# A gated MLP's up-projection as seven half-size products instead of eight

## The chip, the cores and the metric

The kernel runs on one core of one Trainium2 chip. The metric is the device time of one execution in microseconds (us); the number for a kernel is the median of its runs. One execution was also taken with the hardware profiler, and every row below is from that one.

## What is computed

Two trunk layers act on 640 tokens (128 context tokens and 512 latent tokens) of width 1024. Each layer is a mixer followed by a gated MLP with a depthwise convolution of width 3 over the tokens between its up-projection and its activation. The part that matters here:

```python
D_FF = ((8 * D_MODEL // 3 + 127) // 128) * 128      # 2816 = 22 chunks of 128
FFN_CONV = 3
...
def conv_ffn(h, p):
    u = dwconv(h @ p['ffn_w_up'], p['ffn_conv_w'], p['ffn_conv_b'])
    val, gate = jnp.split(u, 2, axis=-1)
    return (jax.nn.silu(gate) * val) @ p['ffn_w_down']
```

All data is fp32. The kernel multiplies with a split: each operand is the sum of a high part in the fp32r format and a low part, and a product is three matmuls (weight high times input high, weight high times input low, weight low times input high) that are accumulated in PSUM.

## The kernel before, in words

The program is written by a planner. Python generators emit the instructions; a class `Clock` keeps an estimated time for each engine, and `pick` gives an elementwise step to whichever of two engines would be through first by those estimates. The estimates hold a cost for each instruction alone. `Engine` records every operation, so that all instructions carry the line of its call (L175) in the profile, and the groups go by tile names.

The main stream is a list of jobs in order. Beside it run threads (`spawn`) that consume the results. `Stream` (`ws`) loads the weights: a unit is 128 x 1024 values; `raw` is its landing place (two buffers, `NRAW`), ScalarE (ACT) makes the high part `wh`, and VectorE (DVE) or GpSimd (POOL) subtracts to make the low part `wl`. There are three buffers of each (`NSPLIT`), loads run up to two units ahead of the splits, and a raw buffer is free again as soon as its one split is done.

In the MLP the normalised input lies feature-major in `h_hi` and `h_lo`: 8 blocks of 128 features by 642 columns (128 context tokens, two zero columns, 512 latent tokens). `up` makes the 44 chunks of 128 output features, a value chunk `j` and then its gate chunk `22 + j`. A chunk is one `fm_job`: 8 blocks times 3 matmuls on two pieces of columns, 258 and 384 wide (`PIECES`), into two PSUM banks, 48 matmuls in all. `up_then` consumes them: `conv` reads the PSUM banks (first tap on ACT or DVE, the two other taps as DVE scalar_tensor_tensor), then Silu on the gate, the product of value and gate, and a split into `act_hi` and `act_lo`. The chunks are made in `GROUPS` of 8, 8 and 6 pairs; after each group `down` (and `down_last`) multiplies its part of the activations with the down weights, in two halves of 512 output columns, and `add_gated` adds the result to the residual. `fm_primed` runs the first chunks of a layer in column stages, as the normalised tiles come.

PSUM has 8 banks, of which up to 6 (`MCAP`) serve products of the main stream.

Of the kernel before, what the change touches and what calls it, by code (L numbers as in the profile page):

```python
# [9 lines left out]
F32 = mybir.dt.float32  # L10
# [5 lines left out]
NT = 642  # L16
EPS = 1e-6
GROUPS = ((0, 8), (8, 16), (16, 22))
# [41 lines left out]
class Clock:  # L60
    """estimated times of the engines, for the order in which instructions are emitted"""
# [49 lines left out]
    def free(self, n):  # L111
        """when the last user of a tile is done"""
# [18 lines left out]
ROWS = {"xT": NT, "s0": 2, "sh0": 2, "h_hi": NT, "h_lo": NT, "C456": 384}  # L131


def tnames(xs):
    """what the waits go by: tiles, or the rows of the tiles that are worked on in parts"""
# [13 lines left out]
class Slots:  # L149
    """a pool whose tiles take over the waits of the tiles that had their place"""  # L150
# [92 lines left out]
def kernel(ctx: ExitStack, tc: tile.TileContext, a: dict, o: dict):  # L243
# [27 lines left out]
    # PSUM tiles and token-major tiles are taken and given back in emission order, so that no engine waits for a later one  # L271
# [4 lines left out]
    def get(kind, n=1, keep=0):  # L276
# [13 lines left out]
        pool = pl["tok" if kind == "tok" else "gn"].real  # L290
# [77 lines left out]
    def slot_free(tag, bufs):  # L368
        """when the next tile of the tag is free"""
        L = strm.names.get(tag, [])  # L370
        return clk.free(L[-bufs]) if len(L) >= bufs else 0.0

    class Stream:
        """units of the products' weights: loads run NRAW ahead of the splits, splits tn.look ahead of the products"""

        def __init__(self):
            self.desc, self.got, self.on = [], {}, False
            self.n_dma = self.n_split = self.n_take = self.n_done = 0

        def pump(self, force=False):  # L380
            while self.on:
                now, i = clk.now(), self.n_split
                if i < min(self.n_dma, self.n_take + tn.look, self.n_done + NSPLIT) and (
                        force or slot_free("wh", NSPLIT) <= now and clk.free(tname(self.got[i])) <= now + 0.5):
                    raw, n = self.got[i], self.desc[i][1]
                    hi = strm.tile([128, 1024], F32R, tag="wh", name="wh", bufs=NSPLIT)
                    lo = strm.tile([128, 1024], F32R, tag="wl", name="wl", bufs=NSPLIT)
                    ACT.activation(hi[:, :n], raw[:, :n], AF.Copy)
                    eng = DVE if pick(clk.last, DVE=n / 960 + tn.lobias, POOL=n / 460) == "DVE" else POOL
                    eng.tensor_tensor(lo[:, :n], raw[:, :n], f(hi[:, :n]), ALU.subtract)  # L390
                    self.got[i] = (hi, lo)
                    self.n_split += 1
                    continue
                i = self.n_dma
                if i < min(len(self.desc), self.n_split + NRAW) and (force or slot_free("raw", NRAW) <= now + 0.5):
                    src, n = self.desc[i]
                    t = strm.tile([128, 1024], F32, tag="raw", name="raw", bufs=NRAW)
                    SP.dma_start(t[:, :n], src)
                    self.got[i] = t
# [11 lines left out]
        def done(self, n=1):  # L411
            self.n_done += n
# [18 lines left out]
    def load_x(key, src):  # L431
        """the residual stream stays out of SBUF while the mixer needs the room"""
# [1476 lines left out]
```

## Time and profile before

| | us |
|---|---|
| median of 3 runs | 1764.34 |
| lowest and highest run | 1763.33, 1765.52 |
| span of the profiled execution, first to last instruction | 1752.2 |
| PE busy in it | 1661.6 |
| DVE, ACT, POOL busy in it | 1009.3, 718.5, 537.4 |

The profiled execution's own time is not given apart from its span; the median lies 12.1 us above the span. PE is TensorE's matmul stream, PEld its weight loads, which overlap it. Matmul records overlap one another, since matmuls are pipelined: the pace of a stretch is read from start to start, not from the length of a record. The MLP of the first layer runs from about 412 to 890 us, that of the second from about 1275 us to the end.

### The profile page before, as it was taken

The numbers are of one execution on the slowest core, as the hardware profiler recorded it, in microseconds if no ns is written. First come the engines' busy times: TensorE is split into PE (matmuls) and PEld (weight loads), VectorE is DVE, ScalarE is ACT, GpSimd is POOL, SyncE is SP. The second block draws the span as 40 slices with busy tenths as digits, with TensorE's granted clock in tenths as the row PEclk, the third lists the DMA queues.
The fourth block names the chain that finished last, engine by engine and source line by source line (L and its number), as shares of the span: only waits on it lengthen the run. The fifth ranks groups of instructions, "written<-read, shape, count | busy, mean of one in ns | idle before, by whom it ended". The sixth has DMA issues, their size and how long they took to land.

```text
span 1752.2 us, 25505 instructions
## 1 busy us (share of the span) xinstructions
PE 1661.6 (95%) x10192; PEld 1485.5 (85%) x10192; DVE 1009.3 (58%) x1866; ACT 718.5 (41%) x1136; POOL 537.4 (31%) x344
## 2 busy tenths in 40 slices
PE   6897999999999999999999899999899999999997
PEld 5787878768997999799789876887799989998996
DVE  5467987677443344344464779877854434443445
ACT  6466435426332233223274765443453313331333
POOL 1334653322331233123123355442213212321331
PEclk9998999999999999999999999999999999999999
DMA  8424555533223222322533355643122321222222
GB/s 326 121 49 81 128 179 174 187 109 103 73 73 108 64 82 73 96 73 73 180 121 107 75 135 158 181 166 105 60 73 73 87 81 61 73 85 72 73 85 84
DMA packets 62668, 188.63 MB, mean 108 GB/s; under 512 B 9550, under 2 KB 17734, under 8 KB 62550
## 3 DMA queue, kind: packets, MB, share of 16 engines
q1 hardware_dynamic: 62550, 187.01, 34.7%
q8 instruction: 80, 1.31, 0.3%
q14 instruction: 38, 0.31, 0.1%
HBM read 180.46 MB, written 6.52 MB: 107 GB/s over the span
## 4 chain that ended last, share of the span: by engine, by line
PE 72%; DVE 14%; ACT 4%; DMA 4%; issue 3%; POOL 1%; SPq 0%; POOLq 0%; DVEq 0%; ACTq 0%
PE at L175 72%; DVE tok L175 5%; DVE x L175 2%; DMA wg<-in_wlru 2%; DVE gt L175 1%; DVE sp L175 1%; DVE C L175 1%; DMA tok<-cTd 1%; ACT L175 1%; DVE lb L175 1%; ACT xn L175 1%; ACT hf L175 1%; POOL wl L175 1%; DMA araw<-in_w_ada 1%; ACT lb L175 1%
## 5 line engine op out<-in xcount | busy, mean ns | idle before, releaser
L175 POOL TENSOR_TENSOR wl<-raw,wh 128x1024 fp32r<-128x1024 f32 (+3 forms) x167 | 388.3, 2326 | 946.7 <-ACT wh L175 883.2
L175 PE MATMUL at<-h_hi,wh 128*128 128x258 f32 (+2 forms) x1912 | 599.9, 314 | 5.0 <-ACT wh L175 3.9
L175 PE MATMUL at<-h_hi,wl 128*128 128x258 f32 (+2 forms) x1912 | 590.4, 309 | 5.6 <-POOL wl L175 4.8
L175 PE MATMUL at<-h_lo,wh 128*128 128x258 f32 (+2 forms) x1912 | 590.0, 309 | 0.5 <-DVE h_lo L175 0.5
L175 PEld LDWEIGHTS at<-h_hi,wh 128*128 128x128 f32 x1912 | 363.7, 190 | 20.1 <-issue 5.2
L175 PEld LDWEIGHTS at<-h_hi,wl 128*128 128x128 f32 x1912 | 362.8, 190 | 6.9 <-POOL wl L175 5.9
L175 PEld LDWEIGHTS at<-h_lo,wh 128*128 128x128 f32 x1912 | 364.1, 190 | 2.6 <-DVE h_lo L175 0.7
L175 ACT ACTIVATE wh<-raw 128x1024 fp32r<-128x1024 f32 (+3 forms) x210 | 212.7, 1013 | 223.1 <-PE at L175 168.1
L175 DVE SCALAR_TENSOR_TENSOR cv<-at,par,cv 128x258 f32<-128x258 f32 (+1 forms) x352 | 185.9, 550 | 71.4 <-ACT cv L175 59.6
L175 ACT ACTIVATE cv<-at,par 128x258 f32<-128x258 f32 (+1 forms) x130 | 76.5, 601 | 317.4 <-PE at L175 317.4
L175 PE MATMUL at<-wh,h_hi 128*128 128x384 f32 (+2 forms) x480 | 184.9, 385 | 2.3 <-DVE tok L175 1.4
L175 PE MATMUL at<-wl,h_hi 128*128 128x384 f32 (+2 forms) x480 | 172.6, 359 | 2.7 <-POOL wl L175 2.7
L175 PE MATMUL at<-wh,act_hi 128*128 128x512 f32 x440 | 174.3, 396 | 0.0
L175 PE MATMUL at<-wl,act_hi 128*128 128x512 f32 x440 | 173.6, 395 | 0.6 <-POOL wl L175 0.6
L175 PE MATMUL at<-wh,act_lo 128*128 128x512 f32 x440 | 173.4, 394 | 0.0
L175 PE MATMUL at<-wh,h_lo 128*128 128x384 f32 (+2 forms) x480 | 172.5, 359 | 0.0
L175 DVE TENSOR_SCALAR cv<-at,par 128x384 f32<-128x384 f32 x46 | 31.2, 677 | 188.3 <-PE at L175 188.3
L175 DVE TENSOR_TENSOR gt<-at,gate 128x512 f32<-128x512 f32 x100 | 68.4, 684 | 104.2 <-PE at L175 104.2
L175 ACT ACT_TABLE_LOAD x87 | 111.6, 1283 | 21.9 <-PE at L175 13.6
L175 PEld LDWEIGHTS at<-wh,h_hi 128*128 128x128 f32 x480 | 91.3, 190 | 28.4 <-issue 12.6
L175 PEld LDWEIGHTS at<-wh,act_hi 128*128 128x128 f32 x440 | 82.7, 188 | 24.0 <-issue 3.4
L175 PEld LDWEIGHTS at<-wl,h_hi 128*128 128x128 f32 x480 | 91.2, 190 | 12.2 <-POOL wl L175 3.5
(169 smaller groups left out, 1903.1 us busy)
## 6 DMA issues: line engine op xcount, KB each, us to landing
raw<-in_wup SPq DMA_DIRECT2D x88, 512.0 KB, 3.5
araw<-in_w_ada SPq DMA_DIRECT2D x80, 512.0 KB, 4.5
raw<-in_wdn SPq DMA_DIRECT2D x44, 512.0 KB, 3.5
raw<-in_wfm SPq DMA_DIRECT2D x28, 512.0 KB, 3.6
ar<-in_wada SPq DMA_DIRECT2D x16, 512.0 KB, 10.2
tok<-cTd SPq DMA_DIRECT2D x40, 192.0 KB, 4.6
raw<-in_wout SPq DMA_DIRECT2D x14, 512.0 KB, 3.5
x<-in_xin SPq DMA_DIRECT2D x10, 512.0 KB
```

Source lines behind the costliest of these rows:

```text
L175: res = real(*args, **kw)
```

## The change

The up-projection of a pair of chunks (value chunk `j` and gate chunk `22 + j`) is done as one 2 x 2 block product. The blocks of the input are two halves of the columns (`NH` = 322; the tiles are widened to 644 columns) by two halves of the features (four blocks of 128 each); the blocks of the weights are the two feature halves by value and gate. The direct way is 8 block products. The new way is the Winograd form of Strassen's product: 7 block products, each of 4 blocks times 3 matmuls on 322 columns.

- `sums` makes the sums of input blocks once per layer, and their splits `s1`, `s2`, `s4` in a new pool `S`; `s3` takes the place of a block of `h_hi` and `h_lo`.
- `Stream.prep` makes the weights of the seven products from the two raw tiles of a pair, half a unit (512 columns) each: four more sums (`T1`, `T2` in two steps, `T4`), and seven splits. The sums are made in place, so both raw tiles stay taken until the last of the seven (`T4`) is prepared; `n_rel` then rises by two and the next two loads may go. Six buffers `w` hold high and low part of one product each.
- `pair_job` runs the seven products in three PSUM banks. Partial results are copied out by ACT (`snap`), added on DVE (`out`) into an SBUF tile `C`, and the accumulation goes on in the same bank.
- The convolution (`conv_sb`) now reads SBUF, with 642 columns at once. `product` is the old product of value and gate.
- The first two pairs of each layer stay as chunks: three in `fm_primed` in both layers (before: two in the first layer, three in the second), and one `fm_job`. 20 pairs per layer go the new way.
- `GROUPS` are now 6, 6, 4 and 6 pairs.

```diff
-GROUPS = ((0, 8), (8, 16), (16, 22))
+GROUPS = ((0, 6), (6, 12), (12, 16), (16, 22))
+NH = 322
...
     class Stream:
+        OPS = ("11", "T1", "T2", "22", "T3", "21", "T4")
...
+        def slot(self, name):
+            self.slots += 1
+            return strm.tile([128, 1024], F32R, tag="w", name=name, bufs=2 * NSPLIT)
+
+        def prep(self, op, i):
...
+            v, g = self.raws[i], self.raws.get(i + 1)
+            t = self.slot("wp")
+            hi, lo = t[:, 0:512], t[:, 512:1024]
+            a, c, b, d = (x_ and x_[:, s_] for x_ in (v, g) for s_ in (slice(0, 512), slice(512, 1024)))
+
+            def tt(*args):
+                (DVE if pick(clk.last, DVE=0.9, POOL=1.25) == "DVE" else POOL).tensor_tensor(*args)
+
+            if op == "T1":
+                src = pl["ffn"].tile([128, 512], F32, tag="t1", name="t1")
+                tt(src, b, a, ALU.subtract)
+            elif op == "T2":
+                tt(b, d, b, ALU.subtract)
+                tt(a, b, a, ALU.add)
+                src = a
+            elif op == "T4":
+                tt(c, c, a, ALU.subtract)
+                src = c
+            else:
+                src = {"11": a, "22": d, "T3": b, "21": c}[op]
+            ACT.activation(hi, src, AF.Copy)
+            eng = DVE if pick(clk.last, DVE=0.6 + tn.lobias / 2, POOL=1.25) == "DVE" else POOL
+            eng.tensor_tensor(lo, src, f(hi), ALU.subtract)
+            if op == "T4":
+                self.n_rel += 2
+                del self.raws[i], self.raws[i + 1]
+            return hi, lo
...
+                    if (last < self.n_dma and self.slots + ns <= self.freed + 2 * NSPLIT
+                            and (self.n_split < self.n_take + (tn.look if op == "w" else 5)) and (
+                            force or slot_free("w", 2 * NSPLIT, ns) <= now
+                            and clk.free(tname(self.raws[last])) <= now + 0.5)):
...
-                if i < min(len(self.desc), self.n_split + NRAW) and (force or slot_free("raw", NRAW) <= now + 0.5):
+                if i < min(len(self.loads), self.n_rel + NRAW) and (force or slot_free("raw", NRAW) <= now + 0.5):
...
+        def sums():
...
+            for t_, k0, c in ((t11, 0, c0), (t12, 4, c0)):
+                tt(t_, f(h_hi[:, k0:k0 + 4, c]), f(h_lo[:, k0:k0 + 4, c]), ALU.add)
...
+            for t_, k0 in ((t22, 4), (t21, 0)):
+                tt(t_, f(h_hi[:, k0:k0 + 4, c1]), f(h_lo[:, k0:k0 + 4, c1]), ALU.add)
...
+            def put(n, src):
+                s_hi, s_lo = S[n]
+                ACT.activation(s_hi, src, AF.Copy)
+                clk.dep = clk.last
+                tt(s_lo, src, f(s_hi), ALU.subtract)
+
+            tt(t22, t22, t21, ALU.add)
+            put("s1", t22)
...
+            tt(cc, t11, t21, ALU.subtract)
+            tt(t11, t22, t11, ALU.subtract)
+            put("s2", t11)
...
+            tt(t12, t12, t11, ALU.subtract)
+            put("s4", t12)
...
+        def conv_sb(dst, src, w):
+            if pick(ACT=0.8, DVE=0.55) == "ACT":
+                ACT.activation(dst, src, AF.Identity, scale=w[:, 1:2], bias=w[:, 3:4])
+            else:
+                DVE.tensor_scalar(dst, src, w[:, 1:2], w[:, 3:4], ALU.mult, ALU.add)
+            yield
+            DVE.scalar_tensor_tensor(dst[:, 1:NT], src[:, 0:NT - 1], w[:, 0:1], dst[:, 1:NT], ALU.mult, ALU.add)
+            DVE.scalar_tensor_tensor(dst[:, 0:NT - 1], src[:, 1:NT], w[:, 2:3], dst[:, 0:NT - 1], ALU.mult, ALU.add)
+
+        def pair_job(j, g0):
...
+            def mul(b, a, start):
+                a_hi, a_lo = S[a]
+                hi, lo = ws.take()
+                ps = bank[b][:, 0:NH]
+                for k in range(4):
+                    for w_, h_, first, last in ((hi, a_hi, k == 0 and start, False), (hi, a_lo, False, False), (lo, a_hi, False, k == 3)):
+                        PE.matmul(ps, w_[:, 128 * k:128 * k + 128], h_[:, k, :], start=first, stop=last, skip_group_check=True)
...
+            def snap(n, b):
+                e = ev[n] = ffn.tile([128, NH], F32, tag=n, name="e")
+                ACT.activation(e, bank[b][:, 0:NH], AF.Copy)
...
+            def out(half, part, b, n, free):
...
+                if n is not None:
+                    DVE.tensor_tensor(dst, src, ev[n][:, 0:w], ALU.add)
...
+                if (half, 1 - part) in ev:
+                    spawn(tail(half))
+
+            def tail(half):
...
+                yield from conv_sb(cc, c, P("cf", l, 22 * half + j))
...
+            bank["P"], = yield from get("mm")
+            yield from mul("P", "a11", True)
+            run_(snap("e1", "P"))
+            bank["V"], = yield from get("mm")
+            yield from mul("V", "s1", True)
+            run_(snap("e5", "V"))
+            yield from after("e1")
+            yield from mul("P", "s2", False)
+            run_(snap("e2", "P"))
+            yield from after("e5")
+            yield from mul("V", "s4", False)
+            run_(out(1, 0, "V", "e2", True))
+            yield from after("e2")
+            yield from mul("P", "s3", False)
+            run_(out(1, 1, "P", "e5", False))
+            bank["Q"], = yield from get("mm")
+            yield from mul("Q", "a12", True)
+            run_(out(0, 0, "Q", "e1", True))
+            yield from after((1, 1))
+            yield from mul("P", "a22", False)
+            run_(out(0, 1, "P", None, True))
```

## Rows read from the trace of the kernel before

**Rows 1.** The page, its first part: busy us, share of the span, instructions.

```profile
PE 1661.6 (95%) x10192; PEld 1485.5 (85%) x10192; DVE 1009.3 (58%) x1866; ACT 718.5 (41%) x1136; POOL 537.4 (31%) x344
```

**Rows 2.** The chain that ended last: start, us, what; its two longest pieces.

```profile
411.99 454.02 PE at L175 x2760
...
1274.83 425.70 PE at L175 x2630
```

**Rows 3.** Busy us by stretch: length, PE, PEld, DVE, ACT, POOL, PEclk, DMA share, GB/s.

```profile
405.00:412.00 7.00, 4.96 (x36) 4.19 (x34) 6.93 (x7) 6.29 (x14) 4.07 (x3) 1.00 0.29 80
...
586.00:643.00 57.00, 57.00 (x387) 57.00 (x386) 25.28 (x44) 17.62 (x25) 16.79 (x7) 1.00 0.27 84
```

**Rows 4.** Timeline of PE, one block of a chunk: start, us, instruction.

```profile
460.13 0.28 PE L175 MATMUL at<-h_hi,wh 128*128 128x258 f32 x1
...
460.48 0.34 PE L175 MATMUL at<-h_hi,wh 128*128 128x384 f32 x1
...
461.01 0.29 PE L175 MATMUL at<-h_hi,wh 128*128 128x258 f32 x1
```

**Rows 5.** Timeline of ACT over one pair of chunks.

```profile
484.70 0.57 ACT L175 ACTIVATE cv<-at,par 128x258 f32<-128x258 f32 x1 [4.96 <-PE at L175]
...
489.92 0.74 ACT L175 ACTIVATE act_hi<-cv 128x642 fp32r<-128x642 f32 x1 [0.89 <-DVE cv L175]
...
498.92 0.57 ACT L175 ACTIVATE cv<-at,par 128x258 f32<-128x258 f32 x1 [4.96 <-PE at L175]
```

**Rows 6.** Timeline of DVE over the same pair.

```profile
486.01 2.18 DVE L175 SCALAR_TENSOR_TENSOR cv<-at,par,cv 128x258 f32<-128x258 f32 x4
...
490.69 0.83 DVE L175 TENSOR_TENSOR act_lo<-cv,act_hi 128x642 fp32r<-128x642 f32 x1 [0.81 <-ACT act_hi L175]
```

**Rows 7.** Timelines of POOL and DVE in two stretches where both work.

```profile
1306.36 2.41 POOL L175 TENSOR_TENSOR wl<-raw,wh 128x1024 fp32r<-128x1024 f32 x1 [4.76 <-ACT wh L175]
...
1305.37 2.19 DVE L175 SCALAR_TENSOR_TENSOR cv<-at,par,cv 128x258 f32<-128x258 f32 x4 [3.08 <-ACT cv L175]
1307.47 1.98 DVE L175 TENSOR_TENSOR act_lo<-cv,act_hi 128x642 fp32r<-128x642 f32 x1
...
399.75 1.19 POOL L175 TENSOR_TENSOR h_lo<-hf,h_hi 128x512 fp32r<-128x512 f32 x1 [21.48 <-ACT h_hi L175]
...
399.84 1.66 DVE L175 TENSOR_TENSOR x<-x,gt 128x512 f32<-128x512 f32 x1
...
401.86 0.69 DVE L175 TENSOR_TENSOR h_lo<-hf,h_hi 128x512 fp32r<-128x512 f32 x1
```

**Rows 8.** By tile and by shape: count, duration ns (min/median/max, or busy and mean).

```profile
L175 DVE SCALAR_TENSOR_TENSOR lb<-lb x16: 818/828/2284, 70.6 to 1076.1; 128x642 f32<-128x642 f32 x16
...
L175 DVE SCALAR_TENSOR_TENSOR cv<-at,par,cv x352: 475/548/622, 426.2 to 1702.9; 128x258 f32<-128x258 f32 x88, 128x383 f32<-128x383 f32 x88
...
L175 DVE TENSOR_TENSOR tok<-tok,at 128x384 f32<-128x384 f32 x28 | 14.2, 547 | 4.6 <-PE at L175 3.9 <-POOL tok L175 0.7
```

**Rows 9.** Timelines of ACT and DVE: a half unit's and a whole unit's split steps.

```profile
411.22 0.63 ACT L175 ACTIVATE h_hi<-hf 128x512 fp32r<-128x512 f32 x1
...
485.16 1.05 ACT L175 ACTIVATE wh<-raw 128x1024 fp32r<-128x1024 f32 x1
...
417.54 1.23 DVE L175 TENSOR_TENSOR wl<-raw,wh 128x1024 fp32r<-128x1024 f32 x1
```

**Rows 10.** DMA issues, KB, us to landing: the page, then 861.9 to 863 us.

```profile
raw<-in_wup SPq DMA_DIRECT2D x88, 512.0 KB, 3.5
...
araw<-in_w_ada SPq DMA_DIRECT2D x2, 512.0 KB, 4.4
raw<-in_wdn SPq DMA_DIRECT2D x1, 512.0 KB, 5.2
```

**Rows 11.** Timeline of PE where an up group ends and down begins.

```profile
699.39 0.34 PE L175 MATMUL at<-h_hi,wl 128*128 128x384 f32 x1
699.57 0.40 PE L175 MATMUL at<-wh,act_hi 128*128 128x512 f32 x1
```

More of the change, by code (lines that the diff above doesn't have):

```diff
@@ L380, in pump @@
         def pump(self, force=False):
             while self.on:
[L382 to L393, printed above, removed]
+                now = clk.now()
@@ L1558, in ffn_jobs, with cv_tile @@
         cur = {}
+        def cv_tile(j, half):
+            while cur.get("mult", -1) < j - 1 if half else cur.get("split", -1) < j - 2:
+                yield
+            return pl["ffn"].tile([128, NT], F32, tag=f"cv{half}", name="cv", bufs=2 - half)
         def up_then(j, g0, half):
             def then(ps, rel_):
-                cc = pl["ffn"].tile([128, NT], F32, tag=f"cv{half}", name="cv", bufs=2)
+                cc = yield from cv_tile(j, half)
                 yield from conv(cc, ps, P("cf", l, 22 * half + j), 1, rel_)
@@ L1569, in then, with product @@
                 yield
-                val = cur["cv", j, 0]
-                DVE.tensor_tensor(val, val, cc, ALU.mult)
-                yield
-                a_hi, a_lo = cur["act", g0]
-                split(a_hi[:, j - g0, :], a_lo[:, j - g0, :], val)
-                yield
-                cur["done", j] = True
-            return then
+                yield from product(j, g0, cur["cv", j, 0], cc)
+            return then
+        def product(j, g0, val, gate):
+            DVE.tensor_tensor(val, val, gate, ALU.mult)
+            cur["mult"] = j
+            yield
+            while ("act", g0) not in cur:
+                yield
+            a_hi, a_lo = cur["act", g0]
+            split(a_hi[:, j - g0, 0:NT], a_lo[:, j - g0, 0:NT], val)
+            cur["split"] = j
+            yield
+            cur["done", j] = True
@@ L1579, in begin_group, with act_tiles @@
+        def act_tiles():
+            return [pl["ffn"].tile([128, 6, 2 * NH], F32R, tag=f"a_{nm}", name=nm) for nm in ("act_hi", "act_lo")]
         def begin_group(g0, g1):
             def fn():
-                cur["act", g0] = [pl["ffn"].tile([128, g1 - g0, NT], F32R, tag=f"a_{nm}", name=nm, padded_shape=[128, 8, NT])
-                                  for nm in ("act_hi", "act_lo")]
-            return fn
+                while g0 == 0 and "sums" not in cur:
+                    yield
+                cur["act", g0] = act_tiles()
+            return fn
@@ L1593, in up @@
-            for j in range(j0, g1):
-                for half in range(1 if g0 == 0 and j == 1 and TUNE[2 * l + 1]["npr"] > 2 else 0, 2):
-                    add_fm(a["wup"][l, 22 * half + j], up_then(j, g0, half))
+                add_fm(a["wup"][l, 23], up_then(1, g0, 1))
+                hook(lambda: cur.update(plain=True))
+            else:
+                hook(lambda: run_now(begin_group(g0, g1)()))
+            for j in range(max(g0, 2), g1):
+                job([("pair", a["wup"][l, j], a["wup"][l, 22 + j])], lambda j=j: pair_job(j, g0))
@@ L1597, in down, with run_now @@
+            if g1 == 22:
+                hook(lambda: pl.exit("S"))
+                hook(lambda: pl.enter("nb", f"nc{l}", side="right"))
+        def run_now(gen):
+            for _ in gen:
+                raise AssertionError
         def down(g0, g1, hf):
```

142 lines of the change are left out of this document (122 added, 20 removed).

## The prediction, made before the changed kernel had been run

> **What bounds the kernel now.** I read the busy shares first, then the chain of waits, then the busy times by stretch, then the timelines of one pair of chunks. PE is busy 1661.6 of 1752.2 us [rows 1], and the two longest pieces of the chain that ended last are PE alone, 454 and 426 us, which are the two MLPs [rows 2]. Inside an up group PE is busy 57.00 of 57.00 us, with DVE at 25.3, ACT at 17.6 and POOL at 16.8 [rows 3]. So in the MLP a shorter matmul stream is worth its full length, as long as the other three engines keep up; they look less than half loaded. A share of 57 us hides which of their steps can run at the same time, and that is where I think this change is decided.
>
> The pace: one block of a chunk, six matmuls, takes 460.13 to 461.01 = 0.88 us, three of 258 columns in 0.35 and three of 384 in 0.53 [rows 4]. That is 0.117 and 0.177 us each, 0.45 and 0.46 ns a column, so time goes with columns. A pair of chunks takes 498.92 - 484.70 = 14.22 us [rows 5].
>
> **PE's part of the change.** A pair had 96 matmuls with 2 x 24 x 642 = 30816 columns; it gets 7 x 12 = 84 with 84 x 322 = 27048. At 14.22 us for 30816 columns that is 12.5 us, or 1.79 for each of the seven products. A width of 322 lies between the two that I can see. 40 pairs would save 40 x 1.74 = 70 us if PE never waited. The Trainium skill (TensorE: Matmul & The Clock Gate, section Back-to-back issue gap) gives an isolated warm gap of N/2.4 + 2.5 ns; by it the saving would be 64 us. The rows are slower than that rule (117 against 110 ns for 258 columns), and I go by the rows.
>
> **The port that DVE and POOL share.** POOL ran a subtraction from 1306.36 for 2.41 us. A DVE subtraction with both inputs in SBUF was issued at 1307.47 and took 1.98 us instead of 0.83: it ended 0.68 us behind POOL's end. The conv steps just before, which have one input in PSUM, ran beside POOL at their usual 2.19 for four. Again at 399.75: POOL 1.19, DVE 1.66 instead of 0.69, ending 0.56 behind [rows 6, 7]. The grouped rows say the same: the conv's step on PSUM never took over 622 ns in 352 cases, the step with two SBUF inputs took 818 to 2284 [rows 8]. So here a POOL subtraction and a DVE step on two SBUF tensors exclude each other for their whole length. The Trainium skill (SBUF — State Buffer, section Who interferes with whom) states this rule, an exclusive lock on a shared port, and it speaks against this change. Without it DVE and POOL would work side by side and the pair would be bound by PE at 12.5; with it the sums below hold. The trace agrees.
>
> Now the pair's steps that need that port. The conv moves from PSUM to SBUF: four 642-wide steps with two SBUF inputs, plus product and activation split as before, six in all, each 0.68 us of port (0.83 as a DVE step) [rows 6 to 8]. Weights: seven low-part subtractions and four sums, eleven half-width steps, 0.56 us of port on DVE (0.69 as a step) or 1.19 on POOL [rows 7]. First taps, if DVE takes them, I count at 0.35. With x of the eleven on DVE the port needs 4.4 + 0.56x + 1.19(11 - x). Before, the same sum was 2 x 0.68 + 2 x 2.41 = 6.2 of 14.2. DVE itself has six steps at 0.83, three adds from PSUM at about 0.5 (547 ns for 384 columns [rows 8]), about 1 of copies and first taps, and 0.69x. x = 11 gives 10.6 of port but 15.1 of DVE; x = 0 gives 17.5 of port. The planner's estimates do not know the port; they favour DVE by 0.15 to 0.35 us when both engines are free, so I take x = 7: 13.1 of port, 12.3 of DVE. No split of the steps lets the pair go at 12.5, and none is far below 13. ACT has seven half-width copies at 0.63, three snaps near 0.6, Silu, split and up to two first taps at 0.74 [rows 5, 9]: at most 9.2, no bound.
>
> **The loop through the raw buffers.** Before, a raw tile came free after one split, and loads ran ahead. Now both tiles of a pair stay taken until T4 is split, and only then go the next two loads. One load lands in 3.5 us, the last of three that were issued together in 5.2 [rows 10]. Then the weight steps follow one another: T1 = 0.69 + 0.63 + 0.69 = 2.0, T2 with two sums 2.7, the splits of 22, T3 and 21 one behind another 1.9, T4 2.0 [rows 7, 9]; with handing over 8.8. The loop is 5.2 + 8.8 = 14.0 us if nothing else is on the port. Six 0.83 steps of the pair that is being multiplied (5.0 us) and POOL's longer steps compete in it; some fall into the load's gap and into T1's, T2's and T4's waits on ACT. Ends: 12.3 (a load of 3.5, nothing else in the way) and 19.0 (all six in the way). I take 16.5, half of the 5.0 in the way, because the DVE queue is in order and the planner, which believes in a shorter loop, puts these steps between each other.
>
> A group's first pair is prepared during the down stage. T4 of its first pair is done at about 4 us (its first product, then 2.0), of the second at 4 + P, and the third pair can run its third product 5.2 + 4.7 behind that, with five products of 1.79 to go: it ends at P + 22.9. A group of six takes 4P + 22.9, one of four 2P + 22.9. Four pairs, six, four and six in each layer: 12P + 91.4. P = 16.5 gives 289 against 20 x 14.25 = 285 before: +9 us for both layers. Ends: P = 14 gives -51, P = 19 gives +69. It breaks even at 16.1.
>
> **From up to down.** Before, PE goes from the last up matmul to the first down matmul without a gap, 699.39 to 699.57 [rows 11]. Now the first down unit is loaded only after the last T4: 3.5 + 1.05 + 2.41 (1.23 on DVE) = 5.8 to 7.0 us [rows 7, 9, 10], while PE has about 4.5 us of products left. Stall 1.3 to 2.5, at eight places, and more if these steps queue: I take 20, ends 0 and 24.
>
> **Head of each MLP.** Twelve sums and subtractions of 1288 columns, by the rows' slope (0.83 at 642, 1.23 at 1024) 1.5 us each on DVE, 3 on POOL; nine of them come after the last norm, 13.6 us, with 9 of conv steps and some 4 of weight steps on the same queue: 26 us. PE covers 72 matmuls of 256 columns (8.5), one chunk (7.1) and three products (5.4): 21. I take 6 a layer, 12 us; ends 0 and 26. The norms there already keep DVE at 6.93 of 7 us [rows 3], so the two early sums do not come free either.
>
> **Other parts, at nothing.** Ten more gate additions a layer (a fourth group) lie beside down matmuls, where PE alone is late; twenty times two steps of 0.69 = 28 us if that cover were gone. Loads are the same bytes. PE's clock: the granted level stayed at 1.00 with PE busy 4.96 of 7 us [rows 3], so PE waits of this size should not lower it.
>
> **Sum.** +9 + 20 + 12 = +41 us. The profiled span is 1752.2; the median lies 12.1 above it and I keep that: 1764.3 + 41 = 1805.
>
> **Rivals.**
> - *The port packs tightly (faster).* T4's steps get through early and the tails fall into the load's gap: P near the port's 13.1, 20 x 13.1 = 261 a layer, -48; half the stalls at the transitions and heads, +16: 1732. Past P = 16.1 it turns. For it: PE's saving is certain, and ACT and the load gap leave room. Against: the measured exclusion.
> - *The queue couples loop and products (slower still).* The last product of a pair accumulates in a bank that `out(1, 1)` must have read on DVE; if that step is queued behind the next pair's first subtraction, which waits for its load, PE waits for a DMA in every pair. P goes to 19: +69 and both upper ends, +119: 1883.
> - *The two sides cancel.* P near 14.5 to 15 (-39 to -27) with the 32 us of stalls: 1757 to 1769, about the old time.
> - *The new width does not pay.* If 322-column matmuls ran at the pace of 384 (0.177 us), PE would need 14.9 a pair; the two widths seen scale, so I give this no chance of its own.
>
> **How the numbers follow.** Forecast case 0.52 (1805; own range 1772 to 1850), slower still 0.12, cancel 0.07, tight 0.29. Within 0.2%, about what a measurement of this kernel can tell from no change, falls nearly all of the cancelling case. So faster 0.30, same 0.07, slower 0.63. The cases have both signs, so the range spans from the tight case's middle to the far end of the slow one: 1728 to 1880.
>
> **What the profile after would show.** Right: in the up groups PE is busy about 75 to 85% and waits for the weight tiles (`wp`, `w`), whose releasers are DVE or POOL subtractions; pairs come every 16 to 17 us; loads of `in_wup` come in twos, each pair of issues just behind a T4 split; DVE steps on `cv` with two SBUF inputs show maxima near 2 us; a gap of 1 to 3 us at each start of down. Wrong: PE busy over 95% there and pairs every 13 us (the tight case), or PE's waits ending at `snap` or `out` rather than at weights, or a gap at the heads of over 15 us.

## The result, and the profile after

| | kernel before | changed kernel |
|---|---|---|
| median, us | 1763.89 (1763.33 to 1765.52, 4 runs) | 1963.78 (1962.13 to 1965.72, 4 runs) |
| span of the profiled execution, us | 1752.2 | 1963.8 |
| ratio of the times, 95% interval | | 1.1134 (1.1118 to 1.115) |

The change costs 200 us. The forecast was 1805 with a range of 1728 to 1880: the sign was right, the size was not.

First the page, its first part, of the changed kernel; [rows 1] is the same line of before.

```profile
PE 1695.1 (86%) x9736; PEld 1465.2 (75%) x9736; DVE 1375.2 (70%) x2269; ACT 832.0 (42%) x1418; POOL 576.9 (29%) x413
```

456 matmuls went, and yet PE is busy 33 us longer; DVE has 366 us more to do. The second group of six pairs shows it by stretch (columns as in [rows 3]: length, PE, PEld, DVE, ACT, POOL, granted clock, DMA share, GB/s):

```profile
585.00:691.00 106.00, 87.72 (x502) 80.26 (x501) 78.11 (x111) 40.70 (x74) 29.68 (x20) 0.94 0.21 65
```

Before, PE filled its stretch and DVE was busy 44% of it [rows 3]. Now six pairs take 106 us, PE stands still for 18 of them, and DVE is busy 74%: 13.0 us a pair, where four pairs of before had 25.3 us together, 6.3 each.

Between first and last matmul of the new products the eight groups take 72.9, 106.8, 69.4, 106.5, 75.8, 108.8, 71.8 and 108.9 us, 720.9 for 40 pairs, 18.0 each. The products themselves are as short as forecast: most of the 3352 steps from one of their matmuls to the next are 148 ns, 1.78 us for twelve. What exceeds 148 ns adds up to 222 us: 85 in waits that end at ACT's copies of a bank (`e`), 62 in waits for high and low parts (`wp`), 13 in waits for DVE's reading of a bank into the tile C (`cc`), 51 in 439 steps of 250 to 290 ns, in which the lower clock was granted, and 11 in others.

The waits of the changed kernel (engine and tile, what ended the wait, us in total, times, longest; `wp` is a high or low part, `raw` and `t` as an engine's output are sums of weight quarters, `e` is ACT's copy of a bank):

```profile
ACT wp L176 <- DVE raw L176: 110.3, 45, 3.9
...
PEld at L176 <- ACT e L176: 96.4, 56, 9.2
...
PE at L176 <- ACT e L176: 81.5, 55, 8.9
...
ACT wp L176 <- POOL raw L176: 64.0, 31, 2.9
...
ACT wp L176 <- DVE t L176: 51.5, 28, 6.7
...
PE at L176 <- ACT wp L176: 33.9, 28, 2.1
...
ACT wp L176 <- POOL t L176: 23.5, 8, 3.4
...
POOL t L176 <- DMA raw<-in_wup: 8.3, 2, 5.7
...
DVE t L176 <- DMA raw<-in_wup: 2.7, 3, 1.3
```

PE waits most for ACT's copies, which looks like a fault of the three-bank scheme. But ACT, busy 42%, itself stands for 249 us ahead of high parts until DVE or POOL has made a sum. And hardly anyone waits for a raw load: 11 us in all.

Where the 211.6 us between the two profiled spans lie, by the start of each layer's first new pair (or the matmul of before that begins the third pair), the end of its last up matmul, and the end:

| | us more than before |
|---|---|
| up to the first pair of layer 0 (442.3, now 462.5) | 20 |
| 40 pairs (571.4, now 720.9) | 150 |
| down stages and what lies between up and down, both layers, with the end | 30 |
| between the last down of layer 0 and the first pair of layer 1 | 12 |

In every run for which both are known the time lies 1.7 to 2.5 us above the span. The profiled execution of the kernel before therefore took about 1754 us, 10 less than the runs in the table at the top, and some 10 of the 211.6 us are a difference between executions and not the work of the change. Part of it lies in the heads: in e1 and e3 below, whose edits do not touch the heads, the first pair of layer 0 starts at 459.1 and 460.8 us.

### The profile page after: what moved, and what is told of

It is laid out like the page before. It is cut to its first block, busy times and chain, and to the rows that moved or that the text cites. A ratio compares the mean times of both kernels' runs of the same rounds, so it can differ in the third digit from the quotient of the medians.

```text
span 1963.8 us, 25516 instructions
## 1 busy us (share of the span) xinstructions
PE 1695.1 (86%) x9736; PEld 1465.2 (75%) x9736; DVE 1375.2 (70%) x2269; ACT 832.0 (42%) x1418; POOL 576.9 (29%) x413
## 5 line engine op out<-in xcount | busy, mean ns | idle before, releaser
L176 PE MATMUL at<-h_hi,wp 128*128 128x322 f32 x1280 | 313.8, 326 | 43.3 <-ACT e L176 22.3
L176 PE MATMUL at<-S,wp 128*128 128x322 f32 x1440 | 267.8, 341 | 96.2 <-ACT e L176 53.9
L176 PEld LDWEIGHTS at<-S,wp 128*128 128x128 f32 x1440 | 237.7, 208 | 123.8 <-ACT e L176 63.4
L176 PEld LDWEIGHTS at<-h_hi,wp 128*128 128x128 f32 x1280 | 227.6, 197 | 63.2 <-ACT e L176 27.4
L176 DVE SCALAR_TENSOR_TENSOR cv<-cc,par,cv 128x641 f32<-128x641 f32 x160 | 193.2, 1207 | 37.5 <-ACT cv L176 34.6
L176 PE MATMUL at<-h_hi,wh 128*128 128x258 f32 (+3 forms) x640 | 207.2, 324 | 13.8 <-ACT wh L176 12.7
L176 PE MATMUL at<-h_hi,wl 128*128 128x258 f32 (+3 forms) x640 | 198.5, 310 | 11.5 <-POOL wl L176 9.4
L176 PE MATMUL at<-h_lo,wp 128*128 128x322 f32 x640 | 205.1, 320 | 0.0
L176 PE MATMUL at<-h_lo,wh 128*128 128x258 f32 (+3 forms) x640 | 197.8, 309 | 1.0 <-DVE h_lo L176 1.0
L176 PEld LDWEIGHTS at<-h_hi,wh 128*128 128x128 f32 x640 | 126.3, 197 | 25.9 <-ACT wh L176 14.5
```

The source lines that it names most:

```text
L176: res = real(*args, **kw)
```

## One wait, followed back

The timeline of ACT in the changed kernel, 602 to 610 us (start, us, instruction, in brackets the idle time before it and what ended it):

```profile
603.11 0.63 ACT L176 ACTIVATE wp<-raw 128x512 fp32r<-128x512 f32 x1 [1.54 <-POOL raw L176]
603.65 0.42 ACT L176 ACTIVATE e<-at 128x322 f32<-128x322 f32 x1
...
608.00 0.74 ACT L176 ACTIVATE act_hi<-cv 128x642 fp32r<-128x642 f32 x1 [3.08 <-DVE cv L176]
608.64 0.61 ACT L176 ACTIVATE wp<-raw 128x512 fp32r<-128x512 f32 x1
609.16 0.42 ACT L176 ACTIVATE e<-at 128x322 f32<-128x322 f32 x1
```

The timeline of PE in the same stretch:

```profile
604.12 4.11 PE L176 MATMUL at<-S,wp 128*128 128x322 f32 x24 [0.39 <-ACT e L176]
609.63 0.42 PE L176 MATMUL at<-h_hi,wp 128*128 128x322 f32 x1 [1.41 <-ACT e L176]
```

And that of DVE:

```profile
604.38 2.72 DVE L176 SCALAR_TENSOR_TENSOR cv<-cc,par,cv 128x641 f32<-128x641 f32 x2
607.13 0.83 DVE L176 TENSOR_TENSOR cv<-cv 128x642 f32<-128x642 f32 x1
```

The 24 matmuls from 604.12 are s2 and s4; s2 was done half way, at about 606.1, and ACT was idle. Its copy of that bank still came only at 609.16, since ahead of it in ACT's queue stood `act_hi`, which waited 3.08 us for the product of value and gate, which stood in DVE's queue behind two outer taps of 2.72 us (0.89 each where POOL is idle; POOL ran a subtraction from 604.66 for 1.75). So PE's s3 started at 609.63. The row names the copy; the time was DVE's, handed on through ACT's queue. At 603.11 the same goes by a weight sum on POOL. What the wait cost afterwards (stretches as above):

```profile
607.00:610.40 3.40, 1.94 (x12) 1.41 (x11) 2.56 (x5) 2.10 (x4) 0.23 (x1) 1.00 0.00 0
610.50:613.90 3.40, 3.40 (x14) 3.40 (x14) 1.82 (x4) 0.63 (x1) 0.95 (x1) 0.51 0.55 154
```

PE had worked 1.94 of the first 3.4 us, and the 3.4 us from 610.5 were granted the 1.2 GHz level (0.51): 14 matmuls in them, where as many us at 148 ns a matmul hold 23.

## The experiments

On the chips of the experiments the kernel before took 1754 to 1756 us. The changed kernel at its ratio of 1.1134 is 1953 us beside it, and that is the figure that the runs are held against. "Pair" is the mean of the 40 pairs, counted as above (e13 and e14: of the 28 pairs in the second and third groups of both layers).

| run | median, us | ratio to before, 95% | pair, us | DVE share, second group |
|---|---|---|---|---|
| changed kernel | 1963.78 (1953 here) | 1.1134 (1.1118 to 1.115) | 18.0 | 74% |
| e1 own banks | 1950.25 | 1.1113 (1.1094 to 1.1133) | 17.1 | 77% |
| e2 no weight sums | 1856.98 | 1.0585 (1.056 to 1.061) | 15.6 | 70% |
| e3 no outer taps | 1879.53 | 1.0713 (1.0684 to 1.0742) | 16.7 | 64% |
| e4 port in the plan | 2073.80 | 1.1828 (1.1805 to 1.1851) | 18.1 | 73% |
| e5 e2 and e3 | 1752.03 | 0.9988 (0.9974 to 1.0002) | 13.4 | 59% |
| e6 e5 and e1 | 1731.57 | 0.9879 (0.9864 to 0.9894) | 12.9 | 59% |
| e7 before, four groups | 1754.33 | 1.001 (0.9996 to 1.0024) | | 46% |
| e8 all on DVE | 1951.68 | 1.1136 (1.1111 to 1.116) | 17.5 | 75% |
| e9 short sums | 1881.72 | 1.0729 (1.0705 to 1.0753) | 16.1 | 70% |
| e10 unread sums | 1934.89 | 1.103 (1.1012 to 1.1047) | 17.4 | 78% |
| e11 unread sums and taps | 1877.90 | 1.0703 (1.0681 to 1.0725) | 16.5 | 83% |
| e12 no operand sums | 1940.75 | 1.1067 (1.1049 to 1.1085) | 17.8 | |
| e13 before, half the load | 1753.84 | 1.0004 (0.9983 to 1.0026) | 14.3 | 73% |
| e14 before, whole load | 1858.85 | 1.0592 (1.0577 to 1.0608) | 15.7 | 88% |

The theories: *snaps* (ACT's copies and the banks that are used twice), *supply or amount* (DVE has too much to do), *port* (DVE and POOL exclude each other, and the plan does not know), *hand-over* (an in-order queue stands until another one has delivered, however short the step).

**e1: a bank for each product.**

```diff
-            yield from after("e1")
-            yield from mul("P", "s2", False)
-            run_(snap("e2", "P"))
+            bank["R"], = yield from get("mm")
+            yield from mul("R", "s2", True)
+            run_(snap("e2", "R"))
...
-            yield from mul("P", "a22", False)
+            bank["Y"], = yield from get("mm")
+            yield from mul("Y", "a22", True)
```

> Each of the seven products of a pair gets a PSUM bank of its own; no product is added on top of a bank that ScalarE has first to copy out, so s2, s4, s3 and a22 no longer wait for the copies e1, e5, e2 and the like. It leaves out the sums of products that were made inside a bank; instructions, weight steps and copies are otherwise the same. Theory snaps (TensorE waits because ScalarE's copies of the banks come late in its in-order queue): the 85 us of matmul steps that end at the copies go, and part of the 51 us at the lower clock with them; the pair falls from 18.0 to about 15 us, the whole to 1830 to 1880 us. Theory supply (sums and low parts on VectorE and GpSimd come late, and the copies are only the place where it shows): the waits move to the weights' high and low parts, the pair stays at 17 us or more, the whole at 1930 to 1965 us.

It gained about 3 us, which the two intervals do not tell from nothing. The largest single group of PE's waits was gone, and time came back at the weights (waits of this run):

```profile
PEld at L176 <- ACT wp L176: 96.4, 61, 5.5
PE at L176 <- ACT wp L176: 77.4, 48, 5.3
...
POOL t L176 <- DMA raw<-in_wup: 55.5, 11, 7.5
```

Before the edit 33.9 us of PE's waits ended at a high part (`ACT wp`), now 77.4. The 40 pairs took 685 us in place of 721, and the down stages with what lies around them 383 in place of 358. So *snaps* falls as the first bound: the copies were the place where PE met a late ACT. POOL's waits for raw loads, 8.3 us in the changed kernel, are 55.5 here.

**e2: no weight sums.**

```diff
-                tt(src, b, a, ALU.subtract)
+                src = b
...
-                tt(b, d, b, ALU.subtract)
-                tt(a, b, a, ALU.add)
...
-                tt(c, c, a, ALU.subtract)
```

> The four sums of weight quarters of each pair (T1, the two of T2, T4) are left out and the products take the bare quarters; the seven high and seven low parts, the copies and the products stay. 160 instructions go, 94 from VectorE and 66 from GpSimd (about 200 us of engine time, of it 100 on VectorE). Theory supply: ScalarE no longer waits for sums in the middle of its queue (174 us of its waits ahead of high parts ended at a sum, 75 at t), so the copies behind them run at once too; the pair falls from 18.0 to 13 to 15 us and the whole to 1820 to 1870 us. Theory snaps (one bank in use twice, whatever the weights do): the waits ahead of s2, s3 and s4 stay near 1 us each, and the whole stays above 1920 us.

96 us less. With nothing changed at the banks, PE's waits for the copies fell from 81.5 to 59.3 us.

**e3: no outer taps.**

```diff
-            DVE.scalar_tensor_tensor(dst[:, 1:NT], src[:, 0:NT - 1], w[:, 0:1], dst[:, 1:NT], ALU.mult, ALU.add)
-            DVE.scalar_tensor_tensor(dst[:, 0:NT - 1], src[:, 1:NT], w[:, 2:3], dst[:, 0:NT - 1], ALU.mult, ALU.add)
```

> The two outer taps of the convolution that now runs out of SBUF are left out (160 instructions on VectorE of 1.2 us, 4.8 us a pair); everything else stays. VectorE's share in a pair falls from 13.3 to about 8.5 us. Theory amount (VectorE simply has too much to do, and what waits behind the taps is late): the pair falls from 18.0 to 14 us or less, the whole to 1800 to 1850 us. Theory snaps: ScalarE's copies and their queue are as they were, the whole falls by less than 40 us, to 1925 to 1960 us. Theory supply by the shared port: the taps are of the kind that stretches beside GpSimd (0.89 us alone, 1.8 us behind it), so most of the gain of the amount comes too, 1830 to 1890 us.

73 us less: under what *amount* expected, over what *snaps* did, and inside the 1830 to 1890 us of the shared port. DVE is at only 64%, so the amount alone is not the whole account; the sums were still awaited here.

**e4: the port in the plan.**

```diff
+        if port:
+            start = max(start, self.port)
...
-        return min(cost, key=lambda e: max(clk.t[e], clk.now() - 1.0, after) + cost[e])
+        pt = clk.port if "DVE" in cost and "POOL" in cost else 0.0
+        return min(cost, key=lambda e: max(clk.t[e], clk.now() - 1.0, after, pt) + cost[e])
```

> The same instructions as the changed kernel, but the planner that sets the order and picks VectorE or GpSimd counts one shared port for GpSimd's work and for VectorE's two-operand work from SBUF. Theory port: the orders were laid out for a VectorE and GpSimd that run side by side and do not; with the port in the plan fewer steps go to GpSimd, the sums come nearer to their due time, and the whole falls by 30 to 80 us, to 1880 to 1935 us. Theory snaps or amount: the same work in the same queues, the whole within 20 us of 1964 us.

121 us slower, which neither theory expected. The plan changed everywhere, and the loss lies outside the up groups: the first pair starts at 513 instead of 462 us, while the 40 pairs take 723.0 against 720.9 us. In the second group POOL's share went from 29.7 to 5.6 us and nothing followed (stretch of this run):

```profile
634.00:740.00 106.00, 86.14 (x498) 79.25 (x497) 77.76 (x127) 40.87 (x73) 5.57 (x4) 0.94 0.20 65
```

**e8: the pairs' sums and low parts on DVE.** The clean form of the same question.

```diff
-                (DVE if pick(clk.last, DVE=0.9, POOL=1.25) == "DVE" else POOL).tensor_tensor(*args)
+                DVE.tensor_tensor(*args)
...
-            eng = DVE if pick(clk.last, DVE=0.6 + tn.lobias / 2, POOL=1.25) == "DVE" else POOL
-            eng.tensor_tensor(lo, src, f(hi), ALU.subtract)
+            DVE.tensor_tensor(lo, src, f(hi), ALU.subtract)
```

> All sums and low parts of the pairs on VectorE, none on GpSimd; the rest of the plan as in the changed kernel. 140 steps of 1.5 us leave GpSimd, VectorE gets as many of 0.69 (about 97 us, 2.4 a pair). Theory port (the two exclude each other on their shared port, so that what GpSimd does there is paid on VectorE in stretched times): VectorE's busy time in a pair stays at 14 us within 0.7, because its work no longer stretches, and the whole stays within 25 us of 1964 us. Theory amount without the port: VectorE goes to 16 us or more in a pair, and the whole rises by 60 to 100 us.

No difference: 1.1136 against 1.1134. The outer taps in the groups by line, of the changed kernel (count, busy us, mean ns, idle time before):

```profile
L176 DVE SCALAR_TENSOR_TENSOR cv<-cc,par,cv 128x641 f32<-128x641 f32 x160 | 193.2, 1207 | 37.5 <-ACT cv L176 34.6
```

The same group in this run:

```profile
L176 DVE SCALAR_TENSOR_TENSOR cv<-cc,par,cv 128x641 f32<-128x641 f32 x160 | 143.6, 898 | 35.1 <-ACT cv L176 32.2
```

And the page of this run:

```profile
PE 1688.2 (87%) x9736; PEld 1455.3 (75%) x9736; DVE 1360.6 (70%) x2393; ACT 845.8 (43%) x1438; POOL 362.5 (19%) x269
```

DVE executes 124 instructions more in 15 us less, since the taps alone shrink by 50 us. What POOL had done on the weights was paid by DVE in stretched steps; POOL's help was worth nothing. The exclusion of [rows 7] is confirmed. The Trainium skill (SBUF — State Buffer, section Who interferes with whom) has the rule, an exclusive lock on the port pair that DVE and POOL share; the trace agrees, 898 against 1207 ns.

**e5 and e6: both amounts away, and the banks too.** The edits are those of e2 and e3 together, and of e1 besides.

> Both things of the second and third run are left out together: the four sums of weight quarters of a pair and the two outer taps of the convolution. VectorE loses about 5.5 us a pair and has 8.6 us or so left. Theory amount (what VectorE and its in-order hand-over with ScalarE can supply sets the pair): the gains add up or nearly (97 and 74 us alone), the pair comes to 13 to 14.5 us and the whole to 1780 to 1825 us, with few matmul steps waiting for high or low parts. Theory of a remaining own cost of the copies and banks: the copies' waits, 59 us of steps after the sums went, stay at 45 us or more, the pair at 15 us or more, and the whole at 1830 to 1860 us.

> As the run before it, and each product in a PSUM bank of its own besides (the sums inside a bank are left out too). Alone the banks were worth 3 us, because the wait moved to the weights. If they are a second bound that lies under the supply, they are worth 25 to 50 us here: pairs of 12.6 to 13 us, the whole 1745 to 1790 us. If the copies were late only because the queue ahead of them was, they are worth under 15 us here too.

The two gains of 96 and 73 us add up to less than the 201 us of e5, which also came out under the 1780 to 1825 us expected. My reading, which no run shows by itself, is that one alone leaves DVE's queue behind PE and both together let it get ahead. The second group's stretch in e5:

```profile
563.00:643.00 80.00, 76.09 (x505) 74.50 (x503) 46.89 (x84) 42.90 (x79) 4.53 (x4) 1.00 0.27 86
```

The same in e6:

```profile
555.00:634.00 79.00, 77.00 (x505) 74.71 (x505) 46.27 (x84) 44.63 (x80) 2.13 (x2) 1.00 0.28 87
```

In e5 12.4 us a pair, the forecast for PE alone, is reached in most pairs of layer 1, and the granted clock in the stretch is back at 1.00. The banks are a second bound, worth 20 us once the supply is there, between the two expectations. They also show what was to be had: with the sums and taps free the whole is as long as before, with the banks free 1.2% shorter. Of the 55 us that the pairs of e6 gain (571.4 to 516.6), 33 are lost again at the heads and around the down stages.

**e7: four groups in the kernel before.**

```diff
-GROUPS = ((0, 8), (8, 16), (16, 22))
+GROUPS = ((0, 6), (6, 12), (12, 16), (16, 22))
```

> The kernel before, with four groups of chunks (6, 6, 4, 6) in place of three (8, 8, 6), and nothing else of the change. The prediction put 12 us on the heads, of them none on the count of groups alone. If the fourth group costs by itself (a primed head, a down stage and its transition more in each layer), the whole rises by 15 to 40 us; the heads of the changed kernel came 28 us late and its down stages ran 15 us longer, which this would then account for. If it costs nothing, the whole is within 6 us of the kernel before.

It costs nothing.

**e9 and e10: time or hand-over.** e9 keeps every sum and every wait and shortens the sums to 32 of 512 columns; e10 keeps the sums' full length on DVE and lets no other engine wait for them. One wait is left: a sum still reads its raw tile, so the next load into that tile waits for it (149 us of the load queue's waits in e10 end at such a sum).

```diff
...
-                tt(c, c, a, ALU.subtract)
+                tt(c[:, 0:32], c[:, 0:32], a[:, 0:32], ALU.subtract)
...
```

```diff
-                (DVE if pick(clk.last, DVE=0.9, POOL=1.25) == "DVE" else POOL).tensor_tensor(*args)
+                DVE.tensor_tensor(*args)
...
-                tt(c, c, a, ALU.subtract)
+                tt(pl["ffn"].tile([128, 512], F32, tag="t1", name="t1"), c, a, ALU.subtract)
...
```

> The four sums of weight quarters stay as instructions with their waits, but each works on 32 of its 512 columns (T1 in place in the third quarter); the rest of the quarters goes bare into the products. All hand-overs of the changed kernel are there, most of the sums' time is not. Base on this chip: the changed kernel 1953 us (1.1134 times the 1754 us of before), without the sums 1857 us. Theory amount (it is VectorE's time that is short): within 25 us of the 1857 us. Theory hand-over (ScalarE stands in the middle of its queue until a sum is done, whatever the sum costs): 1910 us or more. Half way, 1882 to 1910 us, means that both count.

> The mirror of it: all four sums are computed in full, on VectorE (that GpSimd's part may go there at no cost was the eighth run), but into a tile that nobody reads; the products take the bare quarters. VectorE's time is as in the changed kernel, and no high or low part waits for a sum. Theory amount: 1930 to 1960 us, as the changed kernel (1953 us on this chip). Theory hand-over: within 25 us of the 1857 us without sums.

Of the 96 us that the sums cost, e9 gives back 71 by taking their time, e10 18 by taking the waiting for them; what is left over no sums at all is 25 and 78 us. The two agree roughly: three quarters or somewhat more is DVE's and POOL's time, the rest the hand-over.

**e11: the taps unread as well.** As e10, with

```diff
+            t1 = pl["ffn"].tile([128, 616], F32, tag="t1", name="t1")
+            DVE.scalar_tensor_tensor(t1, src[:, 0:616], w[:, 0:1], src[:, 1:617], ALU.mult, ALU.add)
...
```

in place of the first outer tap, and its mirror in place of the second.

> As the run before it, and the two outer taps too go into that unread tile (616 of 641 columns). VectorE has all of its work, 13 to 14 us a pair, and neither a sum nor an outer tap is awaited by a semaphore; what stands behind them in VectorE's own queue still waits. Without both the whole was 1752 us. Theory amount: 1920 to 1960 us, VectorE's work alone does nearly all of the 200 us. Theory hand-over: 1750 to 1830 us.

1878, between the two. Of the 201 us from e5 to the changed kernel, work that no other engine waits for brings back 126, the waiting 75. The raw loads still wait for the unread sums (92 us of the load queue's waits), so 126 is rather too much for DVE's work alone, and 75 rather too little for the hand-over. DVE was busy 83% here, the changed kernel reaches 74% with awaited work.

**e12: no operand sums at the heads.**

```diff
-            for t_, k0, c in ((t11, 0, c0), (t12, 4, c0)):
-                tt(t_, f(h_hi[:, k0:k0 + 4, c]), f(h_lo[:, k0:k0 + 4, c]), ALU.add)
...
-            tt(t22, t22, t21, ALU.add)
-            put("s1", t22)
...
-            put("s3", cc[:, :, 0:NT - NH])
```

> The sums and splits of the token side (s1 to s4, made once a layer at its head out of 1288 columns a step) are left out; the products take bare quarters of the normed tokens. The heads of the changed kernel came 18 and 10 us later than before, where 6 each had been forecast. If the sums stand in the way of the first pair, the heads lose 20 to 30 us and the whole comes to 1920 to 1935 us on this chip (the changed kernel: 1953). If the heads are late because the first pair's weight steps and the norms share VectorE, the whole stays above 1940 us.

12 us less in the whole, on the line between the two expectations. The head of layer 0, the 22 us up to the first pair, in the changed kernel:

```profile
440.00:462.00 22.00, 14.99 (x95) 13.88 (x93) 12.25 (x18) 11.39 (x16) 14.36 (x7) 0.77 0.11 36
```

And in this run:

```profile
427.00:449.00 22.00, 22.00 (x175) 20.93 (x174) 9.20 (x15) 7.57 (x11) 6.41 (x4) 1.00 0.26 84
```

Without the sums PE's hole just ahead of the pairs closes. The first pair of layer 0 comes at 449.0 us, 13 sooner than in the changed kernel and 7 later than before; layer 1's head comes 9 sooner, 2 later than before. So of the 32 us of both heads about 9 remain. The whole gained only 12, since part of the difference is the one between executions named above and the down stages with what lies around them took 364 us here, 358 there.

**e13 and e14: DVE's load in the kernel before.** Passes over 641 columns into an unread tile, two or four behind the convolution of each chunk; the plan also holds a chunk back until the pair two before it has been multiplied or split:

```diff
+                while cur.get("mult" if half else "split", -1) < j - 2:
+                    yield
...
                 yield from conv(cc, ps, P("cf", l, 22 * half + j), 1, rel_)
+                for _ in range(4):
+                    junk = pl["ffn"].tile([128, 641], F32, tag="junk", name="junk")
+                    DVE.scalar_tensor_tensor(junk, cc[:, 0:641], epsb, cc[:, 1:642], ALU.mult, ALU.add)
...
```

> The kernel before, eight products, with VectorE work added that nobody reads: behind each up-projection chunk's convolution two passes over 641 columns into an unread tile (0.89 us each in the changed kernel where GpSimd is idle, 3.6 us for a pair of chunks). VectorE goes from 6.7 to 10.2 us of a pair of 14.25 us (72%). Theory amount: below the 75 to 89% at which the runs so far stopped, so the whole rises by less than 30 us over the 1754 us of before. Theory that any delay in VectorE's queue is paid in full: 60 us or more.

> As the run before it, with four passes a chunk (7.1 us a pair): VectorE has 13.8 us for a pair of 14.25 us (97%), as much as in the changed kernel, without a weight sum, a copy between products or a product in halves. Theory amount: VectorE gets no further than 83 to 89% busy with unawaited work, the pair goes to 15.5 to 16.6 us and the whole to 1805 to 1850 us. Theory hand-over (the waits of the seven-product scheme cost, not VectorE's time): within 25 us of the 1754 us of before.

Two passes cost nothing measurable, four cost 103 us. The stretch of [rows 3] in e13, columns as there:

```profile
586.00:643.00 57.00, 57.00 (x387) 57.00 (x386) 41.87 (x57) 16.77 (x24) 16.82 (x7) 1.00 0.25 78
```

The second group's stretch in e14:

```profile
603.00:731.00 128.00, 119.30 (x770) 116.61 (x768) 112.94 (x139) 34.23 (x49) 21.70 (x9) 0.97 0.21 67
```

At 73% PE does not notice DVE; where the load would have been 97% of PE's time, DVE stops at 88% and the pair grows from 14.3 to 15.7 us (16.0 in this group). Of the 103 us 66 lie in the 40 pairs and 40 in the down stages and what lies around them. No product in halves, no sum and no copy between products is in this kernel, so a load like this on DVE is by itself enough for a loss half as large. That does not show it to be half of the changed kernel's: here too awaited steps stand behind the unread ones in DVE's queue.

## Why the prediction was right or wrong

Right were these steps: 1.79 us a product (1.78 measured), 12.5 us a pair for PE alone (12.4 in e5), the exclusion on the port, x = 7 of 11 weight steps on DVE (298 of 440, 7.45 a pair), the PE share of 75 to 85% in the up groups (83%), four groups at nothing (e7), and that no split between DVE and POOL helps (e8). The sign was right too, but in good part by luck: 32 of the forecast's 41 us were stalls around the pairs, and the pairs, put at +9, brought 150. The Trainium skill's rule for an isolated warm gap (TensorE: Matmul & The Clock Gate, section Back-to-back issue gap), N/2.4 + 2.5 ns, gives an estimate of 137 ns for 322 columns; the rows gave 148, and the measurement decides.

The account of the profiled spans, forecast against measured:

| step | forecast | measured |
|---|---|---|
| pairs | +9 | +150 |
| heads (with what lies between the layers) | +12 | +32 |
| from up to down, down stages, end | +20 | +30 |
| sum | +41 | +212 |
| median above the span | 12 kept | 0 |

Some 10 of the 12 us in the last row are the difference between executions described with the result.

1. **The lead of a group's first pairs.** This is the step that failed most. The formula of a group, (n - 2)P + 22.9, gave the first two pairs 22.9 us between them, since their weights are prepared during the down stage. Measured are 33.6 to 40.2 us, 35.2 on average: 98 of the 141 us that the pairs are off. T4 was to be ready at 4 us for the first pair and at 4 + P = 20.5 for the second. In the six groups that follow a down stage its high part is done at 6.2 to 7.4 and at 28.2 to 29.6 us. So only a group's first pair is early, and not by much (13.8 us in layer 0, 16.5 or 16.6 in layer 1; at the heads 17.3 and 24.6), and the second already goes at the slow pace. In the second group the trace has the first pair's T4 sum (589.4 us) in DVE's queue behind gate additions of the down stage, and the second's T1 (599.2) behind two outer taps, about 4 us after its load had landed (issued at 591.5, with 3.5 us to landing). What the lead would be without them was not tried by itself.
2. **P from the wrong loop.** 16.5 was argued from the loop through the raw buffers; the other 24 pairs take 18.3 each, another 43 us. That the value is near is luck: the waits for raw loads are 11 us in the whole run, in e8 2.8 us with a pair at 17.5, and e5, with the same loads and the same two buffers but without the sums that lengthen the loop, goes at 12.4. The loop is also looser than I had it. Both tiles do not stay taken until T4: in the trace one is loaded again as soon as T3 is split, in the second group 3.3 to 6.0 us ahead of the other (585.5 and 591.5, 610.3 and 613.6 us). Two numbers that I had already written down stood at PE's own 12.5: DVE 12.3 and port 13.1. I read them as a floor that a pair can sit on. The runs that take work off DVE or put it on (e2, e3, e9, e14) move the pace, so it is DVE's load and its hand-over that set it. In no run here did DVE come that near to full: 64 to 77% with awaited steps, 78 to 88% with unawaited ones.
3. **"ACT at most 9.2, no bound".** Its busy time was near (about 8 a pair), its queue was not looked at. It stood 249 us behind sums, and PE's copies stood behind it (the wait followed back above). e11 puts the hand-over at some 75 of 201 us.
4. **The sign "waits ending at `snap`".** I had named it as a sign that the supply theory is wrong. It appeared, and the supply of weights was late all the same: e1 removed those waits and gained 3 us. The releaser in a row of waits was here the last link, not the cause. The sign on the loads did not come: they went one by one, as said under 2, and not in twos behind T4.
5. **The clock.** I had expected no effect of waits of this size. 439 steps at the lower level cost 51 us, as a consequence: in e6 36 steps are left.
6. **Heads.** 6 us a layer had been forecast, 20 and 12 came, some of it the difference between executions. Without the operand sums (e12) 7 and 2 are left, so most of it is theirs; the whole gained 12 us by it. **Transitions** were too high (20; PE's gaps from up to down are 2.5, 1.6, 1.6 and 0.6 us in layer 0 and nearly none in layer 1). Instead the down stages themselves take 340 us against 317.5; in e5, with DVE relieved, 324.
7. **The rivals.** *The queue couples* had the time nearest, by a mechanism that was not there: waits at a22 for `out(1, 1)` are 5 us in all. None of the cases let the hand-over and DVE's load add to each other, and so the range ended at 1880, which left out even that rival's own 1883.

What stays open: why e4's plan loses 120 us outside the MLPs was not followed, and the 9 us of the heads that are not operand sums have no experiment. A third raw buffer, which would have tested the loop directly, was not tried for want of room in SBUF. The loop may well be the next bound under DVE's: POOL's waits for raw loads rise to 55.5 us in e1 and to 32.4 in e9.

No version that beats both came out of it. Even with sums and outer taps left out the seven products only draw level, and e6, which leaves out more, is 1.2% ahead; a complete kernel would have to take some 5 us a pair off DVE just to draw level.

## What to carry to other kernels

Price the engine that receives the new elementwise work before the engine that is relieved: here 1.7 us of matmuls a pair were bought with 7 us on an in-order engine. Unread work on that engine began to cost somewhere between 73 and 88% of its time (e13, e14); where another in-order queue awaits its results, 64% was already too much (e3). When the largest wait names a short step on a half idle engine, look at what stands ahead of that step in its queue, and test it by removing the wait: if the time only moves to the next name, the cause is further up. Two causes in one queue need not add (96 and 73 us alone, 201 together): take both away in one run before judging either.

## What the runs showed of the hardware

- POOL beside DVE brought nothing here on steps with two SBUF inputs: 140 steps of about 1.5 us on POOL, or the same on DVE, gave 1.1134 and 1.1136 of the time before. An outer tap took 0.90 us with POOL off the weights, 1.21 on average with it.
- DVE at 73% of a stretch cost PE nothing (e13); at 88% a pair took 16.0 us instead of 14.3 (e14).
- A stretch of 3.4 us with PE busy for 1.94 was followed by one at the lower granted level (0.51). In the kernel before, 7 us with PE busy for 4.96 [rows 3] were followed by 6 us at 1.00 (412 to 418 us).
